# Held loads, two plain pairs and one operation for the low sums in a two-layer decoder trunk

## The chip, the cores and the metric

The kernel runs on one core of a Trainium2 chip. The metric is the device time of one execution in microseconds (us), the median of several runs. PE is the matrix engine, DVE, ACT and POOL are the vector, scalar and GpSimd engines, SP issues most of the loads. A load that POOL issues goes through POOL's own queue. Each engine runs its instructions in the order in which they were placed at build time and waits at the first one that isn't ready.

## The reference

Input x is 256 tokens of 2048 features in fp32. Two layers are applied, each with a token mixer and a feed-forward network, then a last norm. Layer 0's mixer is an mLSTM in chunks, layer 1's a recurrent block with a short convolution; the change touches neither.

```python
def swiglu(x, w_in, w_out):
    g, u = jnp.split(x @ w_in, 2, axis=-1)
    return (jax.nn.silu(g) * u) @ w_out

for layer in range(DEPTH):          # DEPTH = 2
    hn = rms_norm(h, norm_mix[layer])
    mix = mlstm_mixer(hn, ...) if layer % 2 == 0 else rglru_mixer(hn, ...)
    h = h + mix
    h = h + swiglu(rms_norm(h, norm_ffn[layer]), ffn_w_in[layer], ffn_w_out[layer])
return rms_norm(h, norm_final)      # w_in 2048 x 11264, w_out 5632 x 2048
```

## The kernel before

**Precision.** Every fp32 product is made of three matmuls of a faster type: both factors are split into a high half (rounded, by a cast on ACT) and a low half (the rest, a subtraction on DVE), and hi·hi, hi·lo and lo·hi are added up in PSUM. For weights the tiles are called whi and wlo; they are made on the chip from the raw tile that a load brings.

**The feed-forward network** (`ffn`) takes most of the time: 397 to 1061 us in layer 0, 1390 to 2050 us and the end in layer 1. Its inner width of 5632 is done in 11 blocks j of 512 columns. A block runs over 8 pairs p of 128-row slices of the weights; a pair's raw tile, 128 x 4 x 512, holds two slices of the gate columns and two of the up columns.

- A *plain* pair uses the tile as it is: one cast and one subtraction of 128 x 2048, then 8 products (24 matmuls of 512 columns).
- A *seven* pair trades a product for additions, as Strassen-Winograd's scheme does: 7 products (21 matmuls). DVE forms four sums t in three operations (L310, L313, L314); ACT casts three raw slices (whix) and the sums in two steps of two (whit); DVE subtracts in one operation (wlox, 128 x 1536) and two (wlot, 128 x 1024 each).

`is_plain(j, p)` says which is which: pair 0 always is plain, in block 0 also those of BOTH; so block 0 has six plain pairs and every other block one. `halves` makes the casts and subtractions. The activations of plain pairs with p above 0 need extra tiles (pool "more"), which is given up after block 0; its room is taken by pool "h1".

**The end of a block.** The four accumulators are combined on DVE and ACT (L865 to L880) into two tiles d0 and s1 of the tile ds. L871 is the operation that first reads Q5, the first accumulator of the end. `turn_v` transposes d0 and s1 on PE (tv), and ACT and DVE split them into hh (L543, L544).

**The second matrix** (`outs`): block j's hh is multiplied by 512 rows of w_out in 8 pieces (q, b) during block j+1 and the start of j+2, in between the pairs. Per q there are two loads: i = 0 by SP into rawo, split by ACT and DVE; i = 1 by POOL into rawo, from which ACT writes its negative into wlo (L928), a second POOL load adds the weights onto it (L929), and ACT casts the high half (L930). A piece's PSUM bank gets h by an ACT copy (L949), collects 12 matmuls, and is copied back to h (L960).

**Order and buffers.** The program is written in one order; a scheduler places the instructions on the engines at build time by its own estimates, data dependences and priority. `with tc.high_priority` lifts the weight halves. Raw, whi and wlo tiles turn over three buffers each (layer openings have one more for raw and whi); a seven pair takes two whi and two wlo tiles, one for x, one for t. The sums have one buffer. The loads of w_out take whatever time they get: nothing but a free buffer keeps a POOL load of block 0's w_out from being issued while block 0 itself begins.

In the order lists below a name carries its place: whit5_7 is block 5, pair 7; whio421 is w_out of block 4, q = 2, i = 1; out420 is block 4's piece q = 2, b = 0.

Of the kernel before, what the change touches and what calls it, by code (L numbers as in the profile page):

```python
# [8 lines left out]
F32 = mybir.dt.float32  # L9
F32R = mybir.dt.float32r  # L10
AF = mybir.ActivationFunctionType
ALU = mybir.AluOpType
# [17 lines left out]
SEVENS = (1, 2, 3, 4, 5, 6, 7)  # L30

BOTH = (1, 2, 3, 4, 7)

SHIFT = 48
PRODUCTS = (
# [9 lines left out]
def kernel(  # L45
# [219 lines left out]
    def split(hi, lo, src):  # L265
        nc.scalar.copy(hi, src)  # L266
        nc.vector.tensor_tensor(lo, src, hi.bitcast(F32), op=ALU.subtract)  # L267

    def halves(name, src, n=4, step=4):

        hi, lo = four("whi", name, F32R, 3), four("wlo", name, F32R, 3)
        for i in range(0, n, step):
            at = slice(i, min(n, i + step))
            split(hi[:, at, :], lo[:, at, :], src[:, at, :])
        return [(hi[:, i, :], lo[:, i, :]) for i in range(n)]

    def stream4(w, c0, nk):
# [9 lines left out]
                yield kg + i, *both[i]  # L287

    def is_plain(j, p):
        return p not in SEVENS or j == 0 and p in BOTH  # L290

    def pairs(w, j, held):

# [514 lines left out]
    def ffn(layer, n, nxt):  # L808
# [85 lines left out]

        fresh, copies = [True], []

        def outs(j, hi, lo):

            wv = ffn_w_out[layer][j * NB:(j + 1) * NB, :].rearrange("(k p) n -> p k n", p=P)
            held = {}

            def load(q, last):
                held.clear() if not last else None
                tiles = held[q] = []
                if last:
                    raw = four("raw", f"o{j}{q}", F32, 2)
                    for i in (0, 2):  # L910
                        nc.sync.dma_start(raw[:, i:i + 2, :], wv[:, i:i + 2, q * NB:(q + 1) * NB])
                    with tc.high_priority(offset=AHEAD):
                        tiles.extend(halves(f"o{j}{q}", raw))
                    return
                for i in range(2):

                    spare = "1" if i and q % 2 else ""
                    raw, wh, wl = (
                        pool_of(f"{what}o{at}").tile([P, 2, NB], dt, tag=f"{what}{i}", name=f"{what}o{j}{q}{i}")
                        for what, dt, at in (("raw", F32, ""), ("whi", F32R, ""), ("wlo", F32R, spare))  # L920
                    )
                    src = wv[:, 2 * i:2 * i + 2, q * NB:(q + 1) * NB]
                    (nc.gpsimd if i else nc.sync).dma_start(raw, src)  # L923
                    with tc.high_priority(offset=AHEAD):
                        if i:

                            with after(*copies[-2:-1]):
                                nc.scalar.activation(wl, raw, AF.Copy, scale=-1.0)  # L928
                            nc.gpsimd.dma_start(wl, src, accum_op=ALU.add)  # L929
                            nc.scalar.copy(wh, raw)  # L930
                        else:
                            split(wh, wl, raw)
                    tiles.extend((wh[:, k, :], wl[:, k, :]) for k in range(2))

            def piece(q, b, last=False):
                if b == 0:
                    load(q, last)
                tiles = held[q]
                bs = slice(b * P, (b + 1) * P)
                hs = h[:, b, q * NB:(q + 1) * NB]  # L940
                name = f"out{j}{q}{b}"
                o = acc(name) if last else pool_of("out").tile([P, NB], F32, tag="out", name=name)


                ends = q == 3 and last and nxt.lag and j == NJ - 1
                first = False if ends else last or fresh.pop() if last or fresh else False
                if not first:
                    with tc.high_priority(offset=AHEAD):
                        nc.scalar.copy(o, hs)  # L949
                for k in range(4):  # L950
                    product(o, (hi[:, k, bs], lo[:, k, bs]), tiles[k], first and k == 0, k == 3, skip_group_check=True)
                if ends:

                    nxt.store(b, o)
                    return
                with tc.high_priority(offset=AHEAD):
                    if first:
                        nc.vector.tensor_tensor(hs, o, hs, op=ALU.add)
                    else:
                        copies.append(nc.scalar.copy(hs, o))  # L960

            return [(piece, q, b) for q in range(4) for b in range(NT)]
# [15 lines left out]

        for j in range(NJ):
            v = inner(j, between)  # L980
            if j == 0:
                close_pools("more")
                open_pool("h1", f"h1_f{layer}")
            both = (pool_of("h1") if j % 2 else fp).tile([P, 2, 4, T], F32R, tag=f"h{j % 2}", name=f"hh{j}")
            hi, lo = both[:, 0], both[:, 1]
            turns.extend(lambda v=v, i=i, hi=hi, lo=lo: turn_v(v, i, hi, lo) for i in range(2))
            late.append(lambda j=j, hi=hi, lo=lo: outs(j, hi, lo))
        turn["raw"] %= 2
        for i, (piece, q, b) in enumerate(work):
            piece(q, b, i >= 2)  # L990
# [239 lines left out]
```

## Time and profile before

| | us |
|---|---|
| median of three runs | 2096.21 |
| lowest and highest run | 2095.6, 2099.12 |
| the profiled execution | 2094.86 |
| its span, first to last instruction | 2093.1 |
| PE busy | 2068.5 |
| DVE busy | 1746.0 |
| ACT busy | 1429.0 |
| feed-forward of layer 0, blocks 0, 1 (L871 to L871) | 45.6, 62.0 |
| feed-forward of layer 1, blocks 0, 1 | 43.5, 62.0 |
| blocks 3 and 4 of layer 0 together | 124.3 |

A row of the windows gives, for a stretch of the span, each engine's busy time with its number of instructions in brackets, the granted PE clock, and the DMA engines. A row of the timeline gives start, duration, engine, line, operation, tiles out<-in, and in square brackets how long the engine was idle before it and what ended that. A row of the waits gives the total, the number and the longest.

### The profile page before, as it was taken

The page shows a single profiled execution, that of the slowest core. Times are in us where ns is not written, and L with a number is a line of the kernel's source. Part 1 is how long each engine was busy: PE and PEld are TensorE (multiplying, and loading weights), DVE is VectorE, ACT ScalarE, POOL GpSimd, SP SyncE. Part 2 cuts the span into 40 slices and gives each one's busy share as a digit, 9 for nine tenths or more (in the row PEclk, how much of TensorE's full clock was granted, in tenths as well). Part 3 has the DMA queues.
Part 4 walks back from the last instruction along what each step waited for, and adds up shares of the span by engine and source line. Part 5 has one row for each costly group of instructions (what it writes and reads, how often), then busy time and mean ns, then how long its engine had stood idle before and what let it go on. Part 6 is the DMA issues. An engine that isn't in the chain of part 4 may idle for free.

```text
span 2093.1 us, 27909 instructions
## 1 busy us (share of the span) xinstructions
PE 2068.5 (99%) x10424; PEld 1738.0 (83%) x10424; DVE 1746.0 (83%) x1930; ACT 1429.0 (68%) x1739; POOL 195.9 (9%) x218
## 2 busy tenths in 40 slices
PE   9999999999999999999999999999999999999998
PEld 8988888877888888888879999887788888888886
DVE  6655556699999999999976787669999999999995
ACT  5444455567777777877864778556787777887775
POOL 0011110000111111111100000000011111111112
PEclk9999999999999999999999999999999999999999
DMA  7556667656878878888765666665787888888784
GB/s 229 170 162 180 181 177 225 187 178 202 254 223 251 234 223 250 241 237 237 224 197 155 191 190 187 219 214 175 218 243 231 242 232 240 242 228 245 231 238 153
DMA packets 223135, 446.66 MB, mean 213 GB/s; under 512 B 16328, under 2 KB 17048, under 8 KB 222872
## 3 DMA queue, kind: packets, MB, share of 16 engines
q1 hardware_dynamic: 189832, 362.02, 53.5%
q0 software_dynamic: 32448, 81.80, 18.1%
q8 instruction: 81, 1.33, 0.3%
q10 hardware_dynamic: 720, 1.07, 0.1%
q14 instruction: 54, 0.44, 0.1%
HBM read 442.74 MB, written 2.10 MB: 213 GB/s over the span
## 4 chain that ended last, share of the span: by engine, by line
PE 73%; DVE 11%; issue 6%; ACT 4%; DMA 4%; POOL 1%; SPq 0%; ACTq 0%; POOLq 0%; DVEq 0%
PE out L829 5%; PE out L830 5%; PE out L831 5%; PE P L830 5%; PE P L831 5%; PE P L829 5%; PE Q L829 4%; PE Q L830 4%; PE Q L831 4%; DMA rawo<-in_ffn_w_out_dram 3%; DVE wlot L267 2%; DVE wlox L267 2%; PE po L328 2%; PE po L327 2%; PE po L326 2%
## 5 line engine op out<-in xcount | busy, mean ns | idle before, releaser
L266 ACT CAST whit<-sum 128x1024 fp32r<-128x1024 f32 x288 | 301.3, 1050 | 182.4 <-DVE sum L310 144.2
L242 DVE TENSOR_TENSOR wlo<-raw,whi 128x1024 fp32r<-128x1024 f32 (+1 forms) x226 | 273.5, 1213 | 172.3 <-ACT whi L241 169.8
L267 DVE TENSOR_TENSOR wlot<-sum,whit 128x1024 fp32r<-128x1024 f32 x288 | 348.9, 1221 | 36.0 <-ACT whit L266 34.6
L241 ACT CAST whi<-raw 128x1024 fp32r<-128x1024 f32 (+1 forms) x226 | 234.5, 1042 | 193.6 <-PE po L328 40.4
L829 PE MATMUL out<-whio,hh 128*128 128x512 f32 x704 | 275.5, 392 | 1.0 <-ACT hh L543 0.5
L830 PE MATMUL out<-wloo,hh 128*128 128x512 f32 x704 | 273.9, 390 | 0.0
L831 PE MATMUL out<-whio,hh 128*128 128x512 f32 x704 | 273.6, 390 | 0.0
L267 DVE TENSOR_TENSOR wlox<-raw,whix 128x1536 fp32r<-128x1536 f32 x144 | 252.5, 1753 | 23.4 <-ACT whix L266 23.0
L266 ACT CAST whix<-raw 128x1536 fp32r<-128x1536 f32 x144 | 213.6, 1483 | 25.4 <-PE P L831 24.2
L310 DVE TENSOR_TENSOR sum<-raw 128x1024 f32<-128x1024 f32 x144 | 176.2, 1223 | 3.9
L929 POOL DMA_DIRECT2D wloo<-in_ffn_w_out_dram x78 | 94.0, 1205 | 702.9 <-ACT wloo L928 678.2
L829 PEld LDWEIGHTS out<-whio,hh 128*128 128x128 f32 x704 | 132.2, 188 | 30.7 <-ACT out L949 1.7
L830 PEld LDWEIGHTS out<-wloo,hh 128*128 128x128 f32 x704 | 132.2, 188 | 28.2 <-DVE wloo L267 0.7
L831 PEld LDWEIGHTS out<-whio,hh 128*128 128x128 f32 x704 | 132.1, 188 | 27.8
L960 ACT COPY h<-out 128x512 f32<-128x512 f32 x154 | 89.8, 583 | 65.3 <-PE out L831 65.2
L923 POOL DMA_DIRECT2D rawo<-in_ffn_w_out_dram x78 | 59.1, 758 | 755.3 <-ACT whio L930 362.6
L267 DVE TENSOR_TENSOR wloo<-rawo,whio 128x1024 fp32r<-128x1024 f32 (+1 forms) x88 | 117.9, 1339 | 4.4 <-ACT whio L266 4.4
L829 PE MATMUL Q<-whit,p_f 128*128 128x512 f32 x288 | 113.9, 400 | 5.2 <-ACT whit L266 4.5
L830 PE MATMUL P<-wlox,p_f 128*128 128x512 f32 x288 | 113.3, 393 | 4.0 <-DVE wlox L267 3.8
L829 PE MATMUL P<-whix,p_f 128*128 128x512 f32 x288 | 112.3, 398 | 2.7 <-ACT whix L266 2.7
L830 PE MATMUL P<-wlot,p_f 128*128 128x512 f32 x288 | 112.6, 391 | 1.7 <-DVE wlot L267 1.7
L830 PE MATMUL Q<-wlot,p_f 128*128 128x512 f32 x288 | 113.2, 397 | 0.1
(296 smaller groups left out, 5240.9 us busy)
## 6 DMA issues: line engine op xcount, KB each, us to landing
raw<-in_ffn_w_in_dram SPq DMA_DIRECT2D x352, 512.0 KB, 4.8
rawo<-in_ffn_w_out_dram SPq DMA_DIRECT2D x98, 512.0 KB, 6.0
raw<-in_m_w_in_dram SPq DMA_DIRECT2D x94, 512.0 KB, 3.8
rawo<-in_ffn_w_out_dram POOLq DMA_DIRECT2D x78, 512.0 KB, 5.9
wloo<-in_ffn_w_out_dram POOLq DMA_DIRECT2D x78, 512.0 KB, 6.4
raw<-in_r_w_in_dram SPq DMA_DIRECT2D x64, 512.0 KB, 3.9
raw<-in_m_w_out_dram SPq DMA_DIRECT2D x32, 512.0 KB, 3.7
raw<-in_r_w_out_dram SPq DMA_DIRECT2D x32, 512.0 KB, 4.2
```

The source lines that it names most:

```text
L241: nc.scalar.copy(hi[:, i:i + step, 0:ncols], r)
L242: nc.vector.tensor_tensor(lo[:, i:i + step, 0:ncols], r, hi[:, i:i + step, 0:ncols].bitcast(F32), op=ALU.subtract)
L266: nc.scalar.copy(hi, src)
L267: nc.vector.tensor_tensor(lo, src, hi.bitcast(F32), op=ALU.subtract)
L310: nc.vector.tensor_tensor(t[:, 0:2, :], raw[:, 1:3, :], raw[:, 3:4, :].broadcast_to([P, 2, NB]), op=ALU.add)
L326: nc.tensor.matmul(o, lhsT=ah[:, bs], rhs=hi, start=(k == 0), stop=False)
L829: nc.tensor.matmul(o, lhsT=a[0], rhs=b[0], start=start, stop=False, **kw)
L830: nc.tensor.matmul(o, lhsT=a[0], rhs=b[1], start=False, stop=False, **kw)
L831: nc.tensor.matmul(o, lhsT=a[1], rhs=b[0], start=False, stop=stop, **kw)
L923: (nc.gpsimd if i else nc.sync).dma_start(raw, src)
L929: nc.gpsimd.dma_start(wl, src, accum_op=ALU.add)
L960: copies.append(nc.scalar.copy(hs, o))
```

## The change

Three edits.

1. Pairs 1 and 3 of block 1 become plain (SECOND). The extra activation tiles for them exist already; their pool is kept for one block more.
2. For block 0's w_out, q = 0, a POOL copy of one element from d0 (`v[0]`) into each of the two raw tiles is put before the loads, so that these can't be issued before block 0's result is there. This is done in both layers. SP and POOL wait with it, since their later instructions stand behind.
3. The low halves of a seven pair's four sums are made by one DVE operation of 128 x 2048 instead of two of 128 x 1024. The casts on ACT stay in two steps. This holds for all seven pairs; there are 140 now, and were 144.

```diff
+SECOND = (1, 3)
...
         hi, lo = four("whi", name, F32R, 3), four("wlo", name, F32R, 3)
         for i in range(0, n, step):
-            at = slice(i, min(n, i + step))
-            split(hi[:, at, :], lo[:, at, :], src[:, at, :])
+            nc.scalar.copy(hi[:, i:min(n, i + step), :], src[:, i:min(n, i + step), :])
+        nc.vector.tensor_tensor(lo[:, 0:n, :], src[:, 0:n, :], hi[:, 0:n, :].bitcast(F32), op=ALU.subtract)
         return [(hi[:, i, :], lo[:, i, :]) for i in range(n)]
...
-        return p not in SEVENS or j == 0 and p in BOTH
+        return p not in SEVENS or j == 0 and p in BOTH or j == 1 and p in SECOND
...
-        def outs(j, hi, lo):
+        def outs(j, hi, lo, v):
...
                     src = wv[:, 2 * i:2 * i + 2, q * NB:(q + 1) * NB]
+                    if j == 0 and q == 0:
+                        nc.gpsimd.tensor_copy(raw[0:1, 0, 0:1], v[0][0:1, 0:1])
                     (nc.gpsimd if i else nc.sync).dma_start(raw, src)
...
             v = inner(j, between)
-            if j == 0:
+            if j == 1:
                 close_pools("more")
                 open_pool("h1", f"h1_f{layer}")
...
-            late.append(lambda j=j, hi=hi, lo=lo: outs(j, hi, lo))
+            late.append(lambda j=j, hi=hi, lo=lo: outs(j, hi, lo, v))
```

The lines of the changed file are two to five higher: L310 is now L312, L314 is L316, the casts and subtractions of `halves` are L275 and L276, L928 is L933, L930 is L935, L949 is L954, L960 is L965.

The scheduler also places other instructions anew. First place: ACT in layer 0's opening, before (whi0_4 is block 0, pair 4; p6 and c are activations):

```order
L266 CAST whi0_4_3846<-raw0_4_3843 128x2048
L266 CAST whi0_3_3815<-raw0_3_3812 128x2048
L928 ACTIVATE wloo001_4207<-rawo001_4205 128x1024
L930 CAST whio001_4206<-rawo001_4205 128x1024
L474 ACTIVATE c_f06_3712<-tr_f06_3707,cols0_96 128x256
L474 ACTIVATE c_f06_3712<-tr_f06_3707,cols0_96 128x2x128
L928 ACTIVATE wloo011_4325<-rawo011_4323 128x1024
L266 CAST whix0_5_3881<-raw0_5_3874 128x1536
```

After, the stretch from the same row, and then the one further on, behind block 0's end:

```order
L275 CAST whi0_4_3846<-raw0_4_3843 128x2048
L275 CAST whi0_3_3815<-raw0_3_3812 128x2048
L476 ACTIVATE c_f06_3712<-tr_f06_3707,cols0_96 128x256
L476 ACTIVATE c_f06_3712<-tr_f06_3707,cols0_96 128x2x128
L275 CAST whix0_5_3881<-raw0_5_3874 128x1536
```

```order
L275 CAST whit1_2_4086<-sum1_2_4078 128x1024
L545 CAST hh0_3993<-tv_4030 128x512
L545 CAST hh0_3993<-tv_4037 128x512
L933 ACTIVATE wloo001_4186<-rawo001_4184 128x1024
L268 CAST whio000_4178<-rawo000_4177 128x1024
L935 CAST whio001_4185<-rawo001_4184 128x1024
L275 CAST whit1_2_4086<-sum1_2_4078 128x1024
L275 CAST whi1_3_4118<-raw1_3_4115 128x2048
```

Both L928 have left the opening; the first now stands behind the casts of hh0, with the second step of whit1_2 three rows behind it.

Second place: DVE at the end of block 5, before:

```order
L267 TENSOR_TENSOR wloo410_6331<-rawo410_6329,whio410_6330 128x1024
L267 TENSOR_TENSOR wlox5_7_6371<-raw5_7_6363,whix5_7_6370 128x1536
L267 TENSOR_TENSOR wlot5_6_6309<-sum5_6_6300,whit5_6_6308 128x1024
L310 TENSOR_TENSOR sum5_7_6366<-raw5_7_6363 128x1024
L313 TENSOR_TENSOR sum5_7_6366<-sum5_7_6366,raw5_7_6363 128x512
L314 TENSOR_TENSOR sum5_7_6366<-sum5_7_6366,raw5_7_6363 128x512
L267 TENSOR_TENSOR wlot5_7_6375<-sum5_7_6366,whit5_7_6374 128x1024 x2
L310 TENSOR_TENSOR sum6_1_6509<-raw6_1_6506 128x1024
L866 TENSOR_TENSOR ds5_5925<-Q6_5_6052,ds5_5925 128x512
```

and after:

```order
L316 TENSOR_TENSOR sum5_6_6255<-sum5_6_6255,raw5_6_6252 128x512
L276 TENSOR_TENSOR wlox5_7_6325<-raw5_7_6317,whix5_7_6324 128x1536
L276 TENSOR_TENSOR wlot5_6_6264<-sum5_6_6255,whit5_6_6263 128x2048
L312 TENSOR_TENSOR sum5_7_6320<-raw5_7_6317 128x1024
L315 TENSOR_TENSOR sum5_7_6320<-sum5_7_6320,raw5_7_6317 128x512
L316 TENSOR_TENSOR sum5_7_6320<-sum5_7_6320,raw5_7_6317 128x512
L276 TENSOR_TENSOR wlo6_0_6386<-raw6_0_6382,whi6_0_6385 128x2048
L276 TENSOR_TENSOR wlot5_7_6329<-sum5_7_6320,whit5_7_6328 128x2048
```

The low half of pair 7's sums (wlot5_7) is one row now, and wlo6_0 of the next block stands ahead of it. In the middle of a block the next pair's wlox stands there in the same way.

ACT at the same place (out410 and out411 are pieces of the second matrix), before and after:

```order
L949 COPY out410_6342<-h_73 128x512
L266 CAST whix5_7_6370<-raw5_7_6363 128x1536
L266 CAST whit5_6_6308<-sum5_6_6300 128x1024
L266 CAST whit5_7_6374<-sum5_7_6366 128x1024
L960 COPY h_73<-out410_6342 128x512
L266 CAST whit5_7_6374<-sum5_7_6366 128x1024
L949 COPY out411_6392<-h_73 128x512
L865 COPY ds5_5925<-P1_5_6020 128x512
```

```order
L275 CAST whix5_7_6324<-raw5_7_6317 128x1536
L275 CAST whit5_6_6263<-sum5_6_6255 128x1024 x2
L965 COPY h_73<-out410_6296 128x512
L933 ACTIVATE wloo421_6418<-rawo421_6416 128x1024
L954 COPY out411_6345<-h_73 128x512
L867 COPY ds5_5885<-P1_5_5979 128x512
L275 CAST whit5_7_6328<-sum5_7_6320 128x1024
L275 CAST whi6_0_6385<-raw6_0_6382 128x2048
L275 CAST whit5_7_6328<-sum5_7_6320 128x1024
L268 CAST whio420_6411<-rawo420_6410 128x1024
L965 COPY h_73<-out411_6345 128x512
L935 CAST whio421_6417<-rawo421_6416 128x1024
```

The cast whi6_0 stands between the two steps of whit5_7 now, and the copy into out420, which is the next row, stands behind both and behind the two casts of whio42.

Third place: PE there, the rows up to the first use of wlot5_7. Before, and after:

```order
L829 MATMUL P4_5_5982<-whit5_6_6308,p6_f0_3719 128x512
L830 MATMUL P4_5_5982<-wlot5_6_6309,p6_f0_3719 128x512
L831 MATMUL P4_5_5982<-whit5_6_6308,p6_f0_3719 128x512
L829 MATMUL P1_5_6020<-whix5_7_6370,p7_f0_3765 128x512
L830 MATMUL P1_5_6020<-wlox5_7_6371,p7_f0_3765 128x512
L831 MATMUL P1_5_6020<-whix5_7_6370,p7_f0_3765 128x512
L829 MATMUL P7_5_6048<-whit5_7_6374,p7_f0_3765 128x512
L829 MATMUL Q6_5_6052<-whit5_7_6374,p7_f0_3765 128x512
L830 MATMUL P7_5_6048<-wlot5_7_6375,p7_f0_3765 128x512
```

```order
L832 MATMUL out411_6345<-wloo411_6291,hh4_5884 128x512
L833 MATMUL out411_6345<-whio411_6290,hh4_5884 128x512
L831 MATMUL Q6_5_6011<-whit5_7_6328,p7_f0_3765 128x512
L831 MATMUL Q3_5_5907<-whix5_7_6324,p7_f0_3765 128x512
L832 MATMUL Q3_5_5907<-wlox5_7_6325,p7_f0_3765 128x512
L833 MATMUL Q3_5_5907<-whix5_7_6324,p7_f0_3765 128x512
L831 MATMUL P4_5_5942<-whit5_7_6328,p7_f0_3765 128x512
L831 MATMUL out420_6423<-whio420_6411,hh4_5884 128x512
L832 MATMUL Q6_5_6011<-wlot5_7_6329,p7_f0_3765 128x512
```

Before, wlot5_7 was used 5 matmuls after the last of pair 6's sums; now 20 matmuls stand in between, among them all of out411 and the first of out420.

## The prediction

> **What bounds the kernel now.** I read the page first: shares of the engines and the chain that ended last.
>
> ```profile
> span 2093.1 us, 27909 instructions
> ...
> PE 2068.5 (99%) x10424; PEld 1738.0 (83%) x10424; DVE 1746.0 (83%) x1930; ACT 1429.0 (68%) x1739; POOL 195.9 (9%) x218
> ...
> PE 73%; DVE 11%; issue 6%; ACT 4%; DMA 4%; POOL 1%; SPq 0%; ACTq 0%; POOLq 0%; DVEq 0%
> ```
>
> PE is the bound, so only two things move the end: how many matmuls there are, and where PE stands still or slow. The table of windows, cut at the operation that closes each block (L871), finds the second kind. The x after PE is its instructions.
>
> ```profile
> core 0: us, PE busy (x) PEld busy (x) DVE busy (x) ACT busy (x) POOL busy (x), PEclk, DMA share, GB/s
> 397.50:443.10 45.60, 43.41 (x186) 35.37 (x187) 33.35 (x37) 28.61 (x29) 4.87 (x5) 0.96 0.76 235
> 443.10:505.10 62.00, 59.44 (x252) 45.16 (x251) 60.07 (x61) 40.19 (x43) 2.71 (x3) 1.00 0.64 197
> ...
> 565.30:689.60 124.30, 123.77 (x552) 101.66 (x551) 117.71 (x116) 96.96 (x111) 15.60 (x16) 1.00 0.84 242
> ...
> 1390.40:1433.90 43.50, 41.92 (x189) 34.29 (x188) 33.45 (x37) 28.64 (x29) 4.72 (x5) 1.00 0.79 241
> 1433.90:1495.90 62.00, 59.33 (x251) 44.71 (x250) 60.05 (x60) 40.14 (x43) 2.70 (x3) 1.00 0.63 201
> ```
>
> The third row is two ordinary blocks: 124.3 / 552 = 0.225 us per PE instruction. At that rate the other four rows should last 41.9, 56.8, 42.6 and 56.5 us. They lost 3.7, 5.2, 0.9 and 5.5: 15.3 us that the two openings give away. In both blocks 1 DVE is busy for 60.1 of 62 us; it is the bound there. Even in ordinary blocks it is busy for 117.7 of 124.3.
>
> The timeline of PE gives its pace and shows the worst stall.
>
> ```profile
> 427.90 0.39 PE L829 MATMUL Q<-whit,p_f 128*128 128x512 f32 x1
> ...
> 430.62 0.39 PE L829 MATMUL P<-whix,p_f 128*128 128x512 f32 x1
> 433.20 0.50 PE L830 MATMUL P<-wlox,p_f 128*128 128x512 f32 x1 [2.19 <-DVE wlox L267]
> ...
> 435.93 0.63 PE L830 MATMUL Q<-wlot,p_f 128*128 128x512 f32 x1
> 436.36 0.63 PE L831 MATMUL Q<-whit,p_f 128*128 128x512 f32 x1
> ...
> 820.90 1.03 PE L889 MATMUL tv<-ident,ds 128*128 128x128 f32 x8
> 821.69 0.48 PE L829 MATMUL P<-whix,p_f 128*128 128x512 f32 x1
> ```
>
> From 427.90 to 430.62 twelve matmuls start, one per 0.227 us; eight transposes take 0.79. An ordinary block has 171 + 96 = 267 matmuls and 8 transposes: 61.3 us of pure PE work, against 62.15 measured (124.3 / 2). So PE stalls for only 0.8 us per ordinary block. After the idle 2.19 us the spacing is 0.43 for some matmuls (435.93 to 436.36), which is the clock of 0.96 in the first window.
>
> **Part 1, the two plain pairs.** Each plain pair has 24 matmuls instead of 21: 2 pairs x 2 layers x 3 = 12 more, 12 x 0.227 = 2.7 us on PE, nothing hides it. DVE loses, per pair, six operations and gains one of 128x2048 (rows of both stand below, in parts 2 and 3): sums 1.22 + 0.69 + 0.69 and low halves 1.75 + 2.46, against 2.28: 4.5 us less, 9 in each block 1, so DVE falls from 60 to 51 there, below PE's work. Block 1's 5.2 and 5.5 us of loss go.
>
> **Part 2, the held loads.** These rows are the opening of the first layer before: the timelines of ACT, DVE and POOL, and the page's table of DMA issues (last figure: us to landing).
>
> ```profile
> 418.38 1.06 ACT L928 ACTIVATE wloo<-rawo 128x1024 fp32r<-128x1024 f32 x1 [8.73 <-DMA rawo<-in_ffn_w_out_dram]
> ...
> 452.02 1.07 ACT L543 CAST hh<-tv 128x512 fp32r<-128x512 f32 x2
> ```
>
> ```profile
> 439.68 2.28 DVE L267 TENSOR_TENSOR wlo<-raw,whi 128x2048 fp32r<-128x2048 f32 x1
> ...
> 446.54 0.74 DVE L880 SCALAR_TENSOR_TENSOR ds<-ds,rstd_f 128x512 f32<-128x512 f32 x1
> ```
>
> ```profile
> 401.14 0.93 POOL L923 DMA_DIRECT2D rawo<-in_ffn_w_out_dram  x1 [104.26 <-ACT junk L386]
> 402.14 0.73 POOL L442 TENSOR_TENSOR rstd_f<-ms_f,mhalf 128x2 f32<-128x2 f32 x1
> ```
>
> ```profile
> rawo<-in_ffn_w_out_dram POOLq DMA_DIRECT2D x78, 512.0 KB, 5.9
> ```
>
> ACT stood for 8.73 us for a w_out load, in front of the casts of pairs 5 and 6; that made wlox late at 433.20. The order now has both L928 behind block 0, so the casts of pairs 5 and 6 follow at once and blocks 0 get their 3.7 and 0.9 back. With parts 1 and 2 all 15.3 us return, less what the hold costs. Its two POOL copies wait for d0 (the first L880). Behind them POOL has only w_out loads; SP issues six raw loads ahead of its first w_out load that stood behind it, and then waits for the copy, with the raw loads of pair 1_5 next, whose buffer comes free only after pair 1_2's sums, later than that. The copies have no row; bounds are 0 and, by the nearest POOL operation, 2 x 0.73; I take the upper, as both stand in one queue. Then 0.93 to issue and 5.9 to land: 8.3 us after d0. ACT reaches L928 after its two hh casts, which before ended 5.8 us after that L880 (452.02 + 1.07 - 447.28). So it waits some 2.5 us, and whit1_2's second half stands four casts behind. By the new order PE needs that pair's low sums 31 matmuls (7.0 us) after the transposes; ACT and DVE need about 1.3 for hh, 2.5 wait, 1.05 + 1.05 + 1.05 + 1.05 for L928, whio, L930 and whit, some 0.3 less for overlaps, and 2.28 for wlot: 10. I take 2.0 as the stall (PE's other work and an earlier hh give some back); bounds 0 and 8.4, the whole landing. Two layers: 4.0 us. whio of the other half waits for SP's load in the same way, and no longer.
>
> **Part 3, one operation for the low sums.** An ordinary block's end before (the seventh of layer 0), by the timelines of DVE, ACT and PE, and one row of the waits.
>
> ```profile
> 789.87 2.46 DVE L267 TENSOR_TENSOR wlot<-sum,whit 128x1024 fp32r<-128x1024 f32 x2
> ...
> 800.01 1.22 DVE L310 TENSOR_TENSOR sum<-raw 128x1024 f32<-128x1024 f32 x1
> 801.15 1.75 DVE L267 TENSOR_TENSOR wlox<-raw,whix 128x1536 fp32r<-128x1536 f32 x1
> 802.82 0.69 DVE L313 TENSOR_TENSOR sum<-sum,raw 128x512 f32<-128x512 f32 x1
> ...
> 806.35 1.23 DVE L267 TENSOR_TENSOR wlot<-sum,whit 128x1024 fp32r<-128x1024 f32 x1 [1.11 <-ACT whit L266]
> ```
>
> ```profile
> 797.67 1.05 ACT L266 CAST whit<-sum 128x1024 fp32r<-128x1024 f32 x1
> 798.62 1.48 ACT L266 CAST whix<-raw 128x1536 fp32r<-128x1536 f32 x1
> 801.32 1.06 ACT L266 CAST whit<-sum 128x1024 fp32r<-128x1024 f32 x1 [1.22 <-DVE sum L310]
> ...
> 806.75 0.58 ACT L865 COPY ds<-P 128x512 f32<-128x512 f32 x1
> 807.22 1.92 ACT L266 CAST whi<-raw 128x2048 fp32r<-128x2048 f32 x1
> ```
>
> ```profile
> 806.37 0.73 PE L829 MATMUL Q<-whit,p_f 128*128 128x512 f32 x2 [0.51 <-ACT whit L266]
> ```
>
> ```profile
> ACT whix L266 <- PE P L831: 24.2, 12, 3.3
> ```
>
> The gain first: two halves in a row take 2.46, one takes 2.28, so 0.18 x 140 pairs = 25 us of DVE at most. But DVE is not what PE waits for in ordinary blocks, so by itself that is worth at most the 0.8 us per block.
>
> The price: the one operation waits for both casts of the sum, and in the new order it stands behind the next pair's wlox, or at a block's end behind the next block's wlo. Three whi buffers serve two tiles per pair, so whix of pair 7 takes the buffer of pair 5's whit and waits until PE has done with pair 5 (the last row is that kind of wait). Count from there, E5. ACT: 0.2 until whix starts, 1.39 to the next start (rows overlap by 0.09), 0.96 and 1.05 for both whit5_6: done at 3.60. DVE: wlot5_6 3.63 to 5.92, sum 5.95 to 7.18. ACT: whit5_7 from 7.23, whi6_0 from 8.19 to 10.11. DVE: wlo6_0 from 10.15, and only then wlot5_7, 12.35 to 14.64. Beside it ACT: whit5_7's other half, whio420, copy of h, whio421, copy into out420: 10.01 + 0.96 + 0.95 + 0.49 + 0.95 + 0.58 = 13.94. PE from E5, by the new order: 34 matmuls to the end of pair 6's sums, 19 more to out420's first (53 x 0.227 = 12.03), one more to pair 7's first low half (12.26). It stands for 1.96 at the former and 0.4 at the latter: 2.4 us in all. The pairs inside a block come out even to within 0.1 us (by the new order PE has 26 matmuls, 5.90 us, between the end of one pair's sums and the next one's low half; the chain above takes 5.92), so I put them at nothing, with up to 0.3 for each of five pairs in the range (18 x 5 x 0.3 = 27). Before, the low half of pair 7 came without wlo6_0 in front, and that place cost the 0.51 of the last PE row.
>
> 2.4 instead of 0.8 is 1.6 per block, in blocks 2 to 10 of two layers: 18 x 1.6 = 28.8 us.
>
> **Sum.** -15.3 + 2.7 + 4.0 + 28.8 = +20.2 us. The profiled execution took 2094.9, so 2115; the median of the runs, 2096.2, is 1.3 above it: 2116.
>
> **Rivals.** *Faster:* the block's end doesn't grow, because ACT or DVE get there earlier than my chain, whose parts were never seen in this order. For it: DVE has 6.6 us of idle time per two blocks. Against: that idle time can't be used where wlot5_7 waits for two casts in a row. Then 2096.2 - 15.3 + 2.7 + 4.0 = 2088, or 2073 if the 0.8 go too (18 x 0.8 = 15). It decides at a stall of 0.8 + 8.6 / 18 = 1.3 us: below that the change gains. [...]
>
> *No change:* a stall near those 1.3 us; 2092 to 2100.
>
> *Half clock:* the 2.4 us also slow the clock, as the 2.19 did at 433.20: eight matmuls at 0.43 instead of 0.227 are 1.6 us, x 18 = 29: 2145. Against: one matmul breaks the stall, and layer 1's opening, which stalled too, kept a clock of 1.00 (fourth row of the windows). [...]
>
> *The hold costs more:* ACT stands for the whole landing in both layers, 8.4 instead of 2.0: 2129. Against: hh comes late anyway.
>
> **How the numbers follow.** Forecast 0.50; half clock 0.11; dear hold 0.05; faster 0.22; no change 0.12. What this kernel's runs can tell from no change is about 0.2% (4 us): slower 0.66, same 0.12, faster 0.22. The range 2083 to 2142 takes in the upper part of the faster case (hold at nothing: 2084) and 0.3 us more per pair; it leaves out about half of the faster case and the tip of the half clock, 0.16 together. The forecast alone spans 2104 to 2130 (stalls of 1.8 to 3.2).
>
> **What would show it.** Right: blocks 0 and 1 last about 42 and 58 to 60 us, no ACT wait of 8 us in the opening, an ordinary pair of blocks about 127.5 us, with waits of PE for wlot or for the copy into out420 at each block's end. Wrong: ordinary blocks still at 62 us, wlot5_7 done before PE asks for it; or PE waiting in block 1 for pair 2's low sums by far more than 2 us.

## The result and the profile after

The changed kernel takes 2191.45 us (median; 2188.19 to 2198.93), the kernel before 2095.47 in the same rounds: a ratio of 1.0463, 95% interval 1.0443 to 1.0482. It is slower, as forecast, but by 96 us, where the prediction had 20. The profiled execution is the longest of the runs (2198.93 us); it took 104 us more than the profiled one of the kernel before (2094.86).

The page of the changed kernel, shares of the engines:

```profile
span 2197.2 us, 27621 instructions
...
PE 2120.1 (96%) x10436; PEld 1750.9 (80%) x10436; DVE 1730.9 (79%) x1770; ACT 1423.8 (65%) x1731; POOL 203.8 (9%) x222
```

DVE is busy for 15 us less, and PE is no longer busy all the time. The windows, cut at the same closing operation as before (L873 now), show where. Rows: block 0, block 1, two ordinary blocks, block 1 of layer 1.

```profile
397.50:440.20 42.70, 42.60 (x190) 34.61 (x190) 33.70 (x35) 25.43 (x25) 0.72 (x1) 1.00 0.56 190
440.20:502.60 62.40, 57.02 (x247) 45.92 (x246) 50.82 (x45) 38.79 (x41) 10.79 (x9) 0.97 0.70 208
570.60:706.70 136.10, 129.90 (x552) 102.42 (x551) 117.91 (x102) 96.89 (x112) 15.58 (x16) 0.97 0.75 215
...
1481.30:1543.60 62.30, 56.99 (x247) 45.86 (x246) 50.75 (x45) 38.77 (x41) 10.66 (x9) 0.97 0.70 207
```

Block 0 went from 45.6 to 42.7 us. Block 1 takes 62.4, against 62.0, although DVE is busy there for only 50.8 us instead of 60.1. Two ordinary blocks take 136.1 instead of 124.3 us for the same 552 PE instructions: 5.9 per block, 106 us in 18 blocks. That is the whole distance of the two profiled executions. DVE is busy for 117.9 us in them, and was for 117.7: the 0.18 us per pair that the one operation should save doesn't show there.

The waits of PE name three places:

```profile
PE Q L832 <- DVE wlot L276: 27.3, 38, 4.8
PE out L831 <- ACT out L954: 27.0, 21, 1.4
PE Q L831 <- ACT whit L275: 13.1, 18, 1.6
```

One ordinary block (the fourth of layer 0) on the timeline of PE: two places in the middle, and the end.

```profile
595.39 0.39 PE L833 MATMUL Q<-whix,p_f 128*128 128x512 f32 x1
596.38 0.50 PE L831 MATMUL Q<-whit,p_f 128*128 128x512 f32 x1 [0.59 <-ACT whit L275]
...
600.59 0.39 PE L833 MATMUL P<-whix,p_f 128*128 128x512 f32 x1
601.76 0.50 PE L832 MATMUL Q<-wlot,p_f 128*128 128x512 f32 x1 [0.77 <-DVE wlot L276]
...
631.46 0.40 PE L831 MATMUL P<-whit,p_f 128*128 128x512 f32 x1
633.27 0.49 PE L831 MATMUL out<-whio,hh 128*128 128x512 f32 x1 [1.42 <-ACT out L954]
634.00 0.50 PE L832 MATMUL Q<-wlot,p_f 128*128 128x512 f32 x1 [0.23 <-DVE wlot L276]
...
635.01 0.63 PE L833 MATMUL P<-whit,p_f 128*128 128x512 f32 x1
635.43 0.63 PE L832 MATMUL Q<-wlot,p_f 128*128 128x512 f32 x1
```

Matmuls start 0.227 us apart when nothing is late. From start to start, less that 0.227, PE loses 0.76 and 0.94 in the middle and 1.58 and 0.50 at the end. Then matmuls start 0.43 apart (last two rows): half clock. The middle is explained by ACT and DVE just ahead of it:

```profile
593.81 1.06 ACT L933 ACTIVATE wloo<-rawo 128x1024 fp32r<-128x1024 f32 x1 [1.84 <-DMA rawo<-in_ffn_w_out_dram]
...
595.29 1.04 ACT L275 CAST whit<-sum 128x1024 fp32r<-128x1024 f32 x1
596.23 1.48 ACT L275 CAST whix<-raw 128x1536 fp32r<-128x1536 f32 x1
```

```profile
594.05 0.69 DVE L316 TENSOR_TENSOR sum<-sum,raw 128x512 f32<-128x512 f32 x1
597.74 1.76 DVE L276 TENSOR_TENSOR wlox<-raw,whix 128x1536 fp32r<-128x1536 f32 x1 [2.99 <-ACT whix L275]
599.41 2.29 DVE L276 TENSOR_TENSOR wlot<-sum,whit 128x2048 fp32r<-128x2048 f32 x1
```

ACT stands for 1.84 us in front of a w_out load with the casts whit and whix behind it; DVE then stands for 2.99 for whix, with wlot behind its wlox. Every ordinary block has such a wait, of 1.5 to 2.9 us, and what PE loses at the first place goes with it: 0.44 behind the shortest (1.52, at 1976.07), 1.79 behind the longest (2.91, at 1908.42).

The opening, on POOL, ACT, DVE and PE:

```profile
445.65 3.96 POOL L927 COPY rawo<-ds 1x1 f32<-1x1 f32 x2 [42.18 <-DVE ds L882]
449.91 0.94 POOL L928 DMA_DIRECT2D rawo<-in_ffn_w_out_dram  x1 [0.31 <-POOL rawo L927]
```

```profile
448.69 1.06 ACT L545 CAST hh<-tv 128x512 fp32r<-128x512 f32 x2
454.61 1.06 ACT L933 ACTIVATE wloo<-rawo 128x1024 fp32r<-128x1024 f32 x1 [4.86 <-DMA rawo<-in_ffn_w_out_dram]
...
457.45 1.04 ACT L275 CAST whit<-sum 128x1024 fp32r<-128x1024 f32 x1
```

```profile
444.75 0.75 DVE L882 SCALAR_TENSOR_TENSOR ds<-ds,rstd_f 128x512 f32<-128x512 f32 x1
...
447.81 1.76 DVE L276 TENSOR_TENSOR wlox<-raw,whix 128x1536 fp32r<-128x1536 f32 x1
...
458.52 2.29 DVE L276 TENSOR_TENSOR wlot<-sum,whit 128x2048 fp32r<-128x2048 f32 x1 [0.61 <-ACT whit L275]
```

```profile
460.87 0.80 PE L832 MATMUL Q<-wlot,p_f 128*128 128x512 f32 x1 [4.80 <-DVE wlot L276]
```

The first DVE row finishes d0. Behind it the two copies of one element took 4.0 us together, ACT waited 4.86 for the load behind them, whit1_2's second half came after that, and PE stood for 4.8 us.

### The profile page after: what moved, and what is told of

Read it like the earlier page. It is cut to its first block, busy times and chain, and to the rows that moved or that the text cites. A ratio compares the mean times of both kernels' runs of the same rounds, so it can differ in the third digit from the quotient of the medians.

```text
span 2197.2 us, 27621 instructions
## 1 busy us (share of the span) xinstructions
PE 2120.1 (96%) x10436; PEld 1750.9 (80%) x10436; DVE 1730.9 (79%) x1770; ACT 1423.8 (65%) x1731; POOL 203.8 (9%) x222
## 4 chain that ended last, share of the span: by engine, by line
issue 46%; PE 43%; POOL 6%; DVE 2%; ACT 2%; DMA 1%; POOLq 0%; ACTq 0%
POOL wloo L934 4%; PE po L330 3%; PE po L328 3%; PE po L329 3%; POOL rawo L928 2%; PE P L832 1%; PE P L833 1%; DMA rawo<-in_ffn_w_out_dram 1%; PE qk L347 1%; PE out L833 1%; PE out L832 1%; PE qk L345 1%; PE qk L346 1%; PE o L330 1%; PE v L328 1%
## 5 line engine op out<-in xcount | busy, mean ns | idle before, releaser
L275 ACT CAST whit<-sum 128x1024 fp32r<-128x1024 f32 x280 | 289.0, 1046 | 73.6 <-PE P L833 45.4
L276 DVE TENSOR_TENSOR wlot<-sum,whit 128x2048 fp32r<-128x2048 f32 x140 | 320.2, 2287 | 18.9 <-ACT whit L275 13.9
L276 DVE TENSOR_TENSOR wlox<-raw,whix 128x1536 fp32r<-128x1536 f32 x140 | 245.9, 1757 | 108.8 <-ACT whix L275 108.5
L831 PE MATMUL out<-whio,hh 128*128 128x512 f32 x704 | 279.7, 397 | 27.0 <-ACT out L954 27.0
L833 PE MATMUL out<-whio,hh 128*128 128x512 f32 x704 | 277.7, 395 | 0.0
L275 ACT CAST whix<-raw 128x1536 fp32r<-128x1536 f32 x140 | 207.2, 1480 | 105.0 <-PE P L833 101.4
L965 ACT COPY h<-out 128x512 f32<-128x512 f32 x154 | 90.0, 585 | 142.7 <-PE out L833 140.5
L312 DVE TENSOR_TENSOR sum<-raw 128x1024 f32<-128x1024 f32 x140 | 170.9, 1221 | 1.9
L832 PE MATMUL Q<-wlot,p_f 128*128 128x512 f32 x280 | 124.6, 445 | 27.3 <-DVE wlot L276 27.3
L831 PE MATMUL Q<-whit,p_f 128*128 128x512 f32 x280 | 114.7, 410 | 13.1 <-ACT whit L275 13.1
L933 ACT ACTIVATE wloo<-rawo 128x1024 fp32r<-128x1024 f32 x78 | 82.9, 1063 | 53.2 <-DMA rawo<-in_ffn_w_out_dram 53.2
L833 PE MATMUL P<-whit,p_f 128*128 128x512 f32 x280 | 117.3, 419 | 0.0
L833 PE MATMUL Q<-whit,p_f 128*128 128x512 f32 x280 | 115.8, 413 | 0.0
L276 DVE TENSOR_TENSOR wlo<-raw,whi 128x2048 fp32r<-128x2048 f32 x36 | 82.3, 2289 | 37.3 <-ACT whi L275 37.3
```

Of the source, the lines that this page charges most:

```text
L275: nc.scalar.copy(hi[:, i:min(n, i + step), :], src[:, i:min(n, i + step), :])
L276: nc.vector.tensor_tensor(lo[:, 0:n, :], src[:, 0:n, :], hi[:, 0:n, :].bitcast(F32), op=ALU.subtract)
L312: nc.vector.tensor_tensor(t[:, 0:2, :], raw[:, 1:3, :], raw[:, 3:4, :].broadcast_to([P, 2, NB]), op=ALU.add)
L831: nc.tensor.matmul(o, lhsT=a[0], rhs=b[0], start=start, stop=False, **kw)
L832: nc.tensor.matmul(o, lhsT=a[0], rhs=b[1], start=False, stop=False, **kw)
L833: nc.tensor.matmul(o, lhsT=a[1], rhs=b[0], start=False, stop=stop, **kw)
```

## The experiments

Theory: the loss belongs to part 3, and there to the order of work that came with the one operation. Rivals: the hold or the plain pairs set that order; the one operation is too late by itself, since it waits for two casts or since it is long. "Kept order" below means that DVE forms a pair's sums ahead of its wlox and ACT casts both halves of them ahead of the next pair's whix. With parts 1 and 2 and without part 3 the order is nearly that in every pair of the ordinary blocks; in the kernel before it isn't everywhere (the table below counts it).

### Each part by itself

Part 3 alone, on the kernel before:

```diff
-            split(hi[:, at, :], lo[:, at, :], src[:, at, :])
+            nc.scalar.copy(hi[:, i:min(n, i + step), :], src[:, i:min(n, i + step), :])
+        nc.vector.tensor_tensor(lo[:, 0:n, :], src[:, 0:n, :], hi[:, 0:n, :].bitcast(F32), op=ALU.subtract)
```

> Part 3 alone: the low halves of a pair's sums in one operation, nothing held, no pair made plain. Theory A (all of the loss of the ordinary blocks belongs to part 3 and to the order of work it brings, the other two parts have no hand in it): blocks 2 to 10 last 67.9 us as in the changed kernel instead of 62.1, 18 x 5.8 = +104, blocks 0 and 1 as before or a little longer: 2195 to 2215 us. Rival B (part 3 alone costs what the prediction said, a longer block end, and the rest comes only together with the other parts): 18 x 1.6 = +29, 2125 us. Rival C (part 3 is a gain by VectorE's time, the loss comes from elsewhere): under 2096 us.

Measured: 2198.76 us, ratio 1.0506 [1.0485, 1.0527]. Part 3 alone costs 104 us, as theory A has it.

Parts 1 and 2, on the changed kernel the same lines the other way round:

```diff
-        nc.vector.tensor_tensor(lo[:, 0:n, :], src[:, 0:n, :], hi[:, 0:n, :].bitcast(F32), op=ALU.subtract)
+            split(hi[:, at, :], lo[:, at, :], src[:, at, :])
```

> Parts 1 and 2 without part 3: two plain pairs in block 1 and the held loads, low halves in two operations as before. Theory A: ordinary blocks stay at 62.1 us; the openings gain what they gave away (15.3) less 2.7 of matmuls less the hold, which in the changed kernel cost a stall of 4.9 us and about 1.6 us of half clock in each layer: 2096 - 15.3 + 2.7 + 13 = 2097 us, or 2088 if the hold's stall is the 2.0 of the prediction. Rival B (the hold or the plain pairs set the order that loses): ordinary blocks at 64 us or more, 2130 to 2195 us.

Measured: 2082.60 us, 0.9938 [0.9924, 0.9953]. Ordinary blocks last 61.6 us, less than the 62.1 of before, so the time lies 5 us below theory A's lower figure. The rival, that the hold or the plain pairs set the order that loses, falls.

Part 1 is that, without the copies as well:

```diff
-                        nc.gpsimd.tensor_copy(raw[0:1, 0, 0:1], v[0][0:1, 0:1])
```

> Part 1 alone: pairs 1 and 3 of block 1 plain, nothing else. By the prediction's step: block 1 gets back 5.2 and 5.5 us, 12 more matmuls cost 2.7, the opening of block 0 stays as it was (3.7 and 0.9 lost): 2096 - 8.0 = 2088 us. Rival (VectorE was not the bound of block 1, the scalar engine's waits for the w_out loads were): block 1 gains nothing and the 24 matmuls of the two layers are added: 2099 us.

Measured: 2074.31 us, 0.9900 [0.9885, 0.9915]: a gain of 20.5 us, more than twice the 8.0 of the prediction's step; the rival had a loss. Its windows: block 1, then the ordinary blocks of either layer.

```profile
443.90:498.20 54.30, 54.30 (x244) 44.87 (x243) 52.37 (x51) 34.68 (x36) 2.47 (x3) 1.00 0.66 203
498.20:1052.70 554.50, 554.50 (x2476) 457.97 (x2476) 531.72 (x511) 438.60 (x496) 69.65 (x72) 1.00 0.83 237
...
1477.80:2032.50 554.70, 554.54 (x2476) 457.85 (x2475) 531.52 (x511) 438.46 (x496) 69.59 (x72) 1.00 0.83 237
```

The same stretches of the kernel before:

```profile
505.10:1061.50 556.40, 552.88 (x2458) 453.43 (x2457) 525.69 (x510) 430.23 (x491) 69.49 (x71) 1.00 0.81 233
...
1495.90:2050.00 554.10, 552.75 (x2458) 453.35 (x2457) 525.94 (x511) 430.03 (x492) 69.49 (x71) 1.00 0.81 234
```

With part 1, PE is never idle in an ordinary block: 554.5 / 2476 = 0.2240 us per instruction. At that rate the 2458 of before should take 550.5 us; they lost 5.9 and 3.6, and that loss went too. Block 1 loses nothing more either.

Part 2 is the copies alone (part 3 undone as above, and the pool given up after block 0 again):

```diff
-        return p not in SEVENS or j == 0 and p in BOTH or j == 1 and p in SECOND
+        return p not in SEVENS or j == 0 and p in BOTH
```

In the next text "the first w_out loads" are those of block 0, q = 0.

> Part 2 alone: the first w_out loads of layer 2 of the block stand behind a copy that waits for the end of block 0. Block 0 gains 3.2 us per layer as in the changed kernel (layer 1 nearer 1), block 1 loses: by the prediction 2.0 us per layer, by the changed kernel's trace 4.9 and 1.6 of half clock. Theory A (the hold's price is set by the two copies and the landing behind them, whatever the rest): 2096 - 4.2 + 13 = 2105 us. Rival (with VectorE the bound of block 1 the stall lies beside VectorE's work and costs nothing): 2092 to 2094 us.

Measured: 2103.26 us, 1.0038 [1.0025, 1.0051]. The hold costs 8.4 us alone, and 8.3 on top of part 1 (2082.60 less 2074.31): its price does not depend on part 1. The rival falls.

Each alone on the kernel before, the parts give -20.5, +8.4 and +104, 92 us in all, where the three together give 96. On top of parts 1 and 2, part 3 costs 109 (2191.45 less 2082.60). The rest is about what is inside the 109.

### Order, wait, or length

First, wlot ahead of the next wlox in DVE's queue:

```diff
+        with after(*sums):
+            ins = nc.vector.tensor_tensor(lo[:, 0:n, :], src[:, 0:n, :], hi[:, 0:n, :].bitcast(F32), op=ALU.subtract)
+        sums[:] = [ins] if name[0] == "t" else []
```

> The whole change, but with the one operation on a pair's sums (wlot) put ahead of the next pair's wlox or the next block's wlo in VectorE's queue, by an order dependency. Theory A (what the prediction priced: the loss is that wlot stands behind the next wlox or wlo): the block's end stalls for 0.8 us or less instead of 2.1, the half clock goes with it, 18 x 3 to 4 us less than the changed kernel: 2120 to 2140 us. Rival B (wlot is late since it waits for both casts of ScalarE, which come after the next pair's whix; VectorE's order matters little): 2180 to 2200 us.

Measured: 2201.07 us, 1.0494 [1.0473, 1.0515]. The clock was almost whole (0.996 against 0.985), and yet ordinary blocks last 68 us: now the largest wait of PE is

```profile
PE Q L836 <- DVE wlot L279: 46.9, 56, 4.9
```

Putting wlot first gains nothing: theory A falls, and the time lies just above the range of rival B, whose reason shows in the trace. DVE's wlot waits there for ACT's whit 122 times, 179.8 us in all, and ACT casts whit behind the next pair's whix in most pairs. It also warns against adding up the losses of a block: without the half clock other stalls took its room.

Second, the wait for both casts with two short operations:

```diff
+        for i in reversed(range(0, n, step)):
+            nc.scalar.copy(hi[:, i:min(n, i + step), :], src[:, i:min(n, i + step), :])
         for i in range(0, n, step):
-            nc.scalar.copy(hi[:, i:min(n, i + step), :], src[:, i:min(n, i + step), :])
-        nc.vector.tensor_tensor(lo[:, 0:n, :], src[:, 0:n, :], hi[:, 0:n, :].bitcast(F32), op=ALU.subtract)
+            at = slice(i, min(n, i + step))
+            nc.vector.tensor_tensor(lo[:, at, :], src[:, at, :], hi[:, at, :].bitcast(F32), op=ALU.subtract)
```

> The whole change, but the low halves of the sums again in two operations of 128x1024, and ScalarE casts the second half of the sums first, so that both operations wait for both casts, as the one operation did. By the emitted order TensorE's matmuls stand as without part 3. Theory A (waiting for both casts is what costs): the first low half comes about 1 us later than with part 3 undone, in each of seven pairs, 2140 to 2190 us. Rival B (the length of the one operation, 2.28 us ahead of the first low half, and the order of matmuls that goes with it, is what costs): as with part 3 undone, 2080 to 2090 us.

Measured: 2082.45 us, 0.9931 [0.9916, 0.9945], the same as with part 3 undone. Waiting for both casts costs nothing in the order that the scheduler then chose, which is that of parts 1 and 2. Length and order were left.

Third, the one operation, whole change, in the kept order:

```diff
+            with after(*casts):
+                last = nc.scalar.copy(hi[:, i:min(n, i + step), :], src[:, i:min(n, i + step), :])
+        casts[:] = [last] if name[0] == "t" else []
+        with after(*(sums if name[0] == "x" else ())):
+            nc.vector.tensor_tensor(lo[:, 0:n, :], src[:, 0:n, :], hi[:, 0:n, :].bitcast(F32), op=ALU.subtract)
...
+                sums[:] = [nc.vector.tensor_tensor(t[:, 3, :], t[:, 2, :], raw[:, 0, :], op=ALU.add)]
```

> The whole change, one operation for the low halves of the sums included, but the order of work kept as it is without part 3 by two order dependencies: a pair's wlox stays behind its three sums on VectorE, and the next pair's whix behind this pair's two whit casts on ScalarE. Theory A (the order that came with the one operation is what costs: the sums stand a pair later, behind the next wlox, and whit behind ScalarE's w_out work): ordinary blocks at 61.6 us again, 2078 to 2086 us as with part 3 undone. Rival B (the one operation itself is too late for TensorE, whatever the order): its first half comes 1.05 us later in seven pairs of each block, so up to 18 x 7 x 1.05 = 132 us more, 2110 to 2215 us.

Measured: 2078.57 us, 0.9925 [0.9912, 0.9939]. With the same operations as the changed kernel it is 113 us faster. It lies 4 us below parts 1 and 2 alone, but the intervals overlap: that the one operation gains by itself is not shown. Its ordinary blocks, and DVE in one of them:

```profile
498.30:1052.80 554.50, 554.50 (x2476) 457.73 (x2476) 529.00 (x447) 437.76 (x496) 69.48 (x71) 1.00 0.84 237
```

```profile
583.24 1.23 DVE L317 TENSOR_TENSOR sum<-raw 128x1024 f32<-128x1024 f32 x1
...
585.23 0.69 DVE L321 TENSOR_TENSOR sum<-sum,raw 128x512 f32<-128x512 f32 x1
585.88 1.76 DVE L281 TENSOR_TENSOR wlox<-raw,whix 128x1536 fp32r<-128x1536 f32 x1
587.79 2.29 DVE L281 TENSOR_TENSOR wlot<-sum,whit 128x2048 fp32r<-128x2048 f32 x1 [0.15 <-PE out L838]
```

In the changed kernel the sums came after wlox and ACT's whit after its w_out work; here the sums fill the time in which ACT makes whix, and whit follows at once. ACT's waits for w_out loads are gone from the ordinary blocks with it; the four that are left stand in the openings. The changed kernel, then this one:

```profile
ACT wloo L933 <- DMA rawo<-in_ffn_w_out_dram: 53.2, 22, 4.9
ACT wloo L938 <- DMA rawo<-in_ffn_w_out_dram: 15.4, 4, 5.7
```

Rival B falls: the one operation is not too late. The order is what costs.

Fourth, the reverse: two operations, as before, but the sums forced behind wlox.

```diff
+                both = halves(f"x{j}_{p}", raw, 3)
+                with after(*wlox):
+                    nc.vector.tensor_tensor(
...
```

> Parts 1 and 2, low halves in two operations as before part 3, but VectorE's first sum of a pair forced behind that pair's wlox, as it stands in the changed kernel (ScalarE's whit casts then come after its w_out work too). Theory A (that order costs by itself): 2110 to 2190 us. Rival B (two operations are short enough to make up for the slipped order): 2080 to 2095 us.

Measured: 2124.96 us, 1.0144 [1.0125, 1.0162], 42 us more than without the force, in ordinary blocks of about 64 us. So that order costs by itself, though less than with the one operation.

The order can be counted in the traces, in the ordinary blocks of both layers. The columns of whit and wlot are about the 108 pairs that have a next pair in their block, the last column about all 126.

| | median us | both whit ahead of the next whix (ACT) | wlot ahead of the next wlox (DVE) | two or three sums ahead of the pair's wlox (DVE) |
|---|---|---|---|---|
| before | 2095.47 | 78 | 78 | 18 |
| part 1 alone | 2074.31 | 108 | 108 | 126 |
| parts 1 and 2 | 2082.60 | 108 | 108 | 126 |
| changed kernel | 2191.45 | 18 | 18 | 18 |
| wlot first | 2201.07 | 18 | 108 | 18 |
| one operation, kept order | 2078.57 | 108 | 108 | 126 |
| two operations, sums behind wlox | 2124.96 | 54 | 54 | 0 |

Only the place of wlot was put back in the fifth row, and nothing was gained; the sixth put back the others too. Which of its two dependencies is needed was not tested.

### The hold, and what could be kept

Parts 1 and 2 with the copies on DVE:

```diff
-                        nc.gpsimd.tensor_copy(raw[0:1, 0, 0:1], v[0][0:1, 0:1])
+                        nc.vector.tensor_copy(raw[0:1, 0, 0:1], v[0][0:1, 0:1])
```

> Parts 1 and 2 without part 3, and the two copies of the hold on VectorE instead of GpSimd. Theory A (the hold costs what GpSimd's two copies take, 1.02 and 2.98 us in the changed kernel, ahead of the load's issue): the load is issued 3 to 4 us earlier, ScalarE waits 1 to 2 us instead of 4.9, both stalls and their half clock go: 2074 to 2077 us. Rival B (the issue and the landing behind d0, 0.9 and 5.9 us, are enough by themselves): 2080 to 2083 us.

Measured: 2078.45 us, 0.9908 [0.9891, 0.9924], some 4 us less than with POOL's copies (the two intervals touch) and between the two theories, but not in the way that theory A says:

```profile
451.57 0.13 DVE L927 COPY rawo<-ds 1x1 f32<-1x1 f32 x1
```

```profile
453.61 0.93 POOL L928 DMA_DIRECT2D rawo<-in_ffn_w_out_dram  x1 [50.47 <-PE P L833]
```

The copy takes 0.13 us, but it was placed late, and the load is issued 3.7 us later than in the changed kernel. ACT's L933 also moved, behind whit1_2 and whi1_3, so that it waits for the load with less behind it that PE needs soon. That this is what helps is argued from the order, not tested.

On part 1 alone, the work on the first w_out tiles behind ACT's copy of P1 (`gate`; it is set in block 0 and counts until the first copy of a piece):

```diff
-                        nc.scalar.copy(s0, ps["P1"])
+                        gate[:] = [nc.scalar.copy(s0, ps["P1"])]
...
-                            with after(*copies[-2:-1]):
+                            with after(*(copies[-2:-1] or gate)):
...
-                            split(wh, wl, raw)
+                            with after(*(() if copies else gate)):
+                                split(wh, wl, raw)
```

> Part 1 alone, and instead of the held loads only ScalarE's and VectorE's work on the first w_out tiles is put behind ScalarE's copy of P1 in block 0; the loads are issued as early as before. Theory A (the opening lost its time because ScalarE stood before a load that had not landed; late work on a landed load costs nothing): block 0 gains the 3 to 4 us that the hold gained in layer 0 and 1 in layer 1, block 1 loses nothing: 2074.3 - 4.5 = 2070 us. Rival B (the three ScalarE operations then crowd block 1, whose ScalarE work already waits for buffers, and push the casts of its first pair): 2074 to 2079 us.

Measured: 2072.89 us, 0.9885 [0.9870, 0.9900]. Block 0 gained 4.4 us and block 1 gave back 2.4, since PE now stood for up to 2.1 us in front of the transposes. Its interval overlaps that of part 1 alone: 2070 was not reached, and a gain over part 1 is not shown.

That and the one operation in the kept order, two diffs shown above together:

> The parts that gained, together: two plain pairs, ScalarE's and VectorE's work on the first w_out tiles behind the copy of P1 (the loads as early as before, no hold), and the one operation in the kept order of the run before. Theory A (TensorE no longer stands in the ordinary blocks, so VectorE's 0.18 us per pair buys nothing): 2070 to 2075 us, as without the one operation. Rival B (VectorE's time still counts at the block ends): 2062 to 2069 us.

Measured: 2082.82 us, 0.9945 [0.9932, 0.9959]: worse than either theory. In the opening the second w_out load's operation had been placed ahead of a silu that ends block 0:

```profile
449.25 1.06 ACT L937 ACTIVATE wloo<-rawo 128x1024 fp32r<-128x1024 f32 x1 [6.43 <-DMA rawo<-in_ffn_w_out_dram]
450.21 0.70 ACT L887 ACTIVATE ds<-ds,rstd_f 128x512 f32<-128x512 f32 x1
```

PE stood for 4.9 us per layer in front of the transposes. The ordinary blocks were at 61.6 as in the others.

The late work without the one operation, and the transposes one pair later:

```diff
-            if left == 0 and p == 0:
+            if left == 0 and p == (1 if j == 1 else 0):
```

> Two plain pairs and the late work on the first w_out tiles, as two runs before, without the one operation; and the transposes of block 0's result come one pair later in block 1 (behind pair 1 instead of pair 0), since TensorE stood there for 2.1 us in each layer until the second tile of that result was done. Theory A (nothing else waits there): both stalls go, 2072.9 - 4.1 = 2069 us. Rival B (the casts of hh and the first products with w_out then come later than TensorE can fill with other matmuls): 2072 to 2080 us.

Measured: 2074.07 us, 0.9898 [0.9882, 0.9915]. The stall moved by a pair (2.0 us for wlo in each layer) instead of going. Rival B holds.

So the versions near 2073 to 2074 us beat the kernel before by about 1%, and all of them rest on part 1.

## Why the prediction was right or wrong

**Part 1: right in kind, too small** (-8.0 on record, -20.5 measured). Block 1 got back what was said (5.6 and 5.8 by the rate of 0.2240). The failing step is the yardstick: 0.225 us per instruction was read from blocks that themselves lost some time, and the loss of ordinary blocks was carried along as a constant (0.8 per block, given up only in the faster rival's 2073). With part 1 the rows of the later blocks, too, were placed in another order (second row of the table above), and 9.5 us of that loss went. Some 2 us of the gain lie outside these rows.

**Part 2: wrong by 9 us** (-4.6 + 4.0 on record, +8.3 measured). Blocks 0 got their time back about as said: in layer 0, 3.8 us by the rate of 0.2240 (45.6 us for 186 PE instructions before, 42.7 for 190 now). The stall in block 1 of the changed kernel was 4.8 us per layer, not 2.0. Two steps failed. The first is ACT's wait, 4.86 instead of 2.5. The copies, priced at 2 x 0.73, took 4.0; issue and landing took 5.0 where 6.8 were put (449.61 to 454.61), so the load came 9.1 us after d0 (445.50) instead of 8.3. The rest is that ACT had done its two casts of hh 4.25 us after d0 (449.75), not 5.8, and stood there the longer. The second is that the working gave 3 us, of which 1 was struck off for work that PE would find; it found none. With ACT's wait as measured, 2.4 longer, the same working gives 3 + 2.4 = 5.4, close to what happened. Half a clock came on top: the rows of blocks 1 show 0.97. With parts 1 and 2 alone, from which the 8.3 comes, ACT's wait was 4.79, the clock stayed whole and PE met the delay as several stalls, the longest of 1.8 us. The rival in which the hold costs more had the right sign and was given 0.05.

**Part 3, the block's end: right** (all of part 3: +28.8 on record, +109 measured on top of the others). 2.4 us were forecast, at out420 and at pair 7's low half; 1.58 and 0.50 were measured at those two places, behind the rows of ACT and DVE that the chain had named.

**Part 3, the pairs inside a block: wrong.** "I put them at nothing" holds only if every load is there on time. The chain had ACT's casts follow each other; ACT in fact stood for 1.84 us at a w_out load in front of them. The two stalls behind that cost 1.7 us per block (0.76 and 0.94), 31 us in 18 blocks, against nothing in the sum and up to 27 that the range allowed.

**Part 3, the clock: the rival came true.** A stretch of half clock follows the stall in 17 of 18 ordinary blocks; eight matmuls at 0.43 instead of 0.227 make 1.6 us, the price on record. It was given 0.11, with the argument that one matmul breaks the stall; the half clock came in spite of that matmul. Two ordinary blocks of the kernel with part 3 alone, in the same order and with the same 277 instructions, bear the price out, one at full clock and one not. Of the 2.1 us between them 0.55 is a longer stall in the middle (1.08 instead of 0.53), the rest is half clock:

```profile
642.40:708.50 66.10, 63.31 (x277) 50.07 (x276) 58.76 (x52) 48.29 (x56) 7.79 (x8) 1.00 0.76 220
...
774.50:842.70 68.20, 64.83 (x277) 51.16 (x276) 58.84 (x51) 48.19 (x56) 7.82 (x8) 0.97 0.74 213
```

2.08 + 1.70 + 1.6 = 5.4 us of an ordinary block's loss; it takes 68.0 us where the kept order takes 61.6, and the last 1.0 is spread over many small gaps. The forecast also priced the operation and its new order as one thing. No step of the working asked what the one operation would cost in the old order, so part 3 looked like a price to pay, and not like 113 us that two dependencies give back. Why the scheduler chose that order stays open.

## What to carry to other kernels

Where a scheduler places the work by its own estimates, a small edit is priced by the rows that it moves, not by the operation that it shortens; hold the old order with a dependency or two, and the edit and the order can be told apart. On an engine that runs in order, whatever waits for a load passes its wait on to all that stands behind: 8.73 us before, 4.86 with the hold, 1.5 to 2.9 in each ordinary block, 6.43 in the last combination, each time ACT at a w_out load. Measure the pace of an engine that is thought to be the bound where nothing is late, or a loss hides in the yardstick.

## What the runs showed of the hardware

**Half clock came in stretches of 3.41 us, all on one grid.** In the changed kernel half clock sets in at 634.54, 702.81 and 771.07, each time for one stretch of 3.41 us; the starts are 68.27 us apart, 20 stretches of 3.413. The 19 stretches from 460.46 to 2153.47, two in the openings and 17 in the ordinary blocks, all start a whole number of 3.413 us apart. Cut at multiples of that length, the windows give:

```profile
631.09:634.50 3.41, 1.76 (x7) 0.93 (x6) 3.41 (x3) 3.41 (x5) 0.74 (x1) 1.00 1.03 383
634.50:637.91 3.41, 3.41 (x9) 2.67 (x9) 3.41 (x5) 0.67 (x2) 0.00 (x0) 0.51 1.04 363
```

and those of the kernel with part 3 alone, at the end of a block with the same stalls (1.60 and 0.49):

```profile
699.22:702.63 3.41, 2.57 (x12) 1.68 (x10) 3.24 (x2) 3.41 (x6) 0.00 (x0) 1.00 1.03 284
702.63:706.04 3.41, 2.61 (x10) 1.96 (x11) 3.41 (x4) 1.94 (x3) 0.74 (x1) 1.00 1.09 387
```

A stretch in which PE was busy for 1.76 us is followed by one at half clock. Where a border cuts the same stall in two (2.57 and 2.61 busy), the clock stays. So stalls that add up to some 1.65 us within one stretch were enough at 17 block ends (PE busy for 1.74 to 1.78 us of the 3.41), and a stall as long can cost nothing more, by its place. The busy time alone does not settle it: a stretch of the changed kernel with 1.78 us was followed by full clock:

```profile
1907.70:1911.11 3.41, 1.78 (x9) 1.15 (x8) 0.58 (x1) 2.69 (x4) 1.21 (x1) 1.00 0.45 135
1911.11:1914.53 3.42, 3.42 (x16) 2.81 (x17) 2.18 (x2) 3.32 (x4) 0.00 (x0) 1.00 1.07 278
```

With parts 1 and 2 PE was busy for 1.64 us from 459.00 to 462.41, and its matmuls behind that stayed 0.22 to 0.24 us apart (463.27 to 465.82); where the stretches of that run begin isn't shown there. In the openings of the changed kernel PE was idle throughout the stretch before the half clock (0.00 busy from 457.05 and from 1498.11); at the block ends it was idle for half its length only.

**A copy of one element on POOL took up to 3 us.** The two copies took 1.02 and 2.98 us in the changed kernel and ended 0.04 us after DVE's wlox (447.81 + 1.76 = 449.57; the copies at 449.61). In layer 1 the same two ends lie 0.05 us apart (1490.60 and 1490.65). With the hold alone the two copies took 5.7 us:

```profile
444.04 5.70 POOL L927 COPY rawo<-ds 1x1 f32<-1x1 f32 x2 [40.34 <-DVE ds L882]
```

What the copies wait for was not tested. On DVE the same copy took 0.13 us.
